# Matmuls on a tile of zeros ahead of and between the first transposes of a two-layer encoder

## The chip, the cores and the metric

The kernel runs on one core of a Trainium2 chip. A core has five engines that run side by side, each with a queue of its own, and tell each other by semaphores when a result is there: TensorE (PE: matmuls and transposes, with weight loads of its own, PEld), VectorE (DVE), ScalarE (ACT), GpSimd (POOL) and SyncE (SP), which issues most of the transfers. TensorE writes to PSUM, a memory of eight banks here, from which VectorE and ScalarE read; everything else lies in SBUF. The metric is the device time of one execution in microseconds (us). The span of a profile goes from the first to the last instruction and is a little shorter.

## The reference

A two-layer encoder over 512 tokens of 1024 channels. Each layer normalizes the tokens, mixes them along the sequence, adds a mixture of 32 experts (top 2 of one group of 8) and a gated embedding. The change lies at the very start of layer 0, in this part:

```python
def rmsnorm(x, g):
    x32 = x.astype(jnp.float32)
    y = x32 * lax.rsqrt(jnp.mean(x32 * x32, axis=-1, keepdims=True) + EPS)
    return (y * g.astype(jnp.float32)).astype(x.dtype)

def short_conv_mixer(xn, w_in, conv_w, w_out):
    bgate, cgate, h = jnp.split(xn @ w_in, 3, axis=-1)
    u = depthwise_conv(cgate * h, conv_w, (1, 1))
    return (bgate * u) @ w_out
...
    h = x
    for i in range(DEPTH):
        xn = rmsnorm(h, norm_mix[i])
```

## The kernel before

The 512 tokens are four token tiles `t` of 128. For each, the start does four things. ScalarE squares the row and sums it in two halves (`square`, L443), GpSimd makes the reciprocal root in three operations of one column (L445, L449, L450), VectorE multiplies row, root and gain in two halves (`normed`, L460), and TensorE transposes 128x128 pieces, four at a time, into an auxiliary PSUM bank (`turned`, L466). Then `turn_dense` splits the bank into two parts that together carry the full precision: ScalarE copies a rounded part (L472), VectorE subtracts it from the bank (L473). The auxiliary banks are a pool of three, `aux`; a bank comes free when L473 has read it. Weights are split likewise, by ScalarE (L147) and VectorE (L158), one half of a loaded slot at a time (`W.pump`).

A product is then three matmuls (`three`, L484 to L486: rounded by rounded, rounded by rest, rest by rounded). `begin` starts the first projection before all tokens are there. It takes two weight tiles and does the product of each with tokens 0 to 255, then with tokens 256 to 511: 24 matmuls of 256 columns in each of the four groups. Through its hook, `arrive(0)` turns token tiles 0 and 1 and issues the normalization of tiles 2 and 3 (`settle(1)`) ahead of the first group; `arrive(1)` turns tiles 2 and 3 between the first group and the second. Nothing reorders an engine's instructions: each queue runs in the order in which the code was written, waits included, so that the second group stands behind all transposes of tiles 2 and 3 on TensorE though it multiplies tokens 0 to 255 alone.

VectorE's queue at this place is: L460 for tile 0 and for tile 1, L473 twice for tile 0, L158, L473 twice for tile 1, L158, L460 for tile 2 and for tile 3, and L473 four times for both. GpSimd's is L445, L449 and L450 for each tile in turn, and ScalarE's: squares of tiles 0 and 1, L472 twice, L147, L472 twice, L147, squares of tiles 2 and 3, L472 four times.

Of the kernel before, what the change touches and what calls it, by code (L numbers as in the profile page):

```python
# [12 lines left out]
BF = mybir.dt.bfloat16  # L13
# [8 lines left out]
P = 128  # L22
# [197 lines left out]
def hybrid_encoder(ctx, tc, A, out):  # L220
    nc = tc.nc
# [7 lines left out]
    bnd = {}  # L229
# [11 lines left out]
    def aux(shape, dt=F32):  # L241
        return psum.tile(shape, dt, name="aux", tag="aux", bufs=3)
# [226 lines left out]
    def turn_dense(t, xn):  # L469
        for a in range(2):  # L470
            ps = turned(xn, a)
            nc.scalar.copy(X.hi[a][:, t], ps)  # L472
            nc.vector.tensor_tensor(X.lo[a][:, t], ps, X.hi[a][:, t], op=ALU.subtract)  # L473
# [774 lines left out]

    W.open(base[:WSP], dense_end[0])
    xns = {}  # L1250

    def arrive(n):
        for t in (2 * n, 2 * n + 1):
            turn_dense(t, xns[t])
            if n == 0:
                W.pump(1)
        if n == 0:
            settle(1)

    def settle(n):  # L1260
        for t in (2 * n, 2 * n + 1):
            square(t, 0)
            square(t, 1)
            xns[t] = normed(t, g0)

    settle(0)
    begin(2, [(0, 2), (2, 4)], arrive)
    W.pump()
    const_setup()
# [136 lines left out]
```

## Time and profile before

| | us |
|---|---|
| median of 3 executions | 1576.45 |
| the three | 1573.3, 1576.45, 1577.18 |
| profiled execution: its time | 1572.59 |
| profiled execution: its span | 1570.6 |
| TensorE busy in the span | 1487.9 (95%) |
| VectorE / ScalarE / GpSimd busy | 691.4 / 375.2 / 183.2 |

TensorE's busy time counts matmuls that overlap in its pipeline as busy, so the 95% say where it waits, not how fast it works. The mean granted clock of the span is 0.991 of full. The longest wait of TensorE in the whole span is the 8.4 us at its start.

### The profile page before, as it was taken

The numbers are of one execution on the slowest core, as the hardware profiler recorded it, in microseconds if no ns is written. First come the engines' busy times: TensorE is split into PE (matmuls) and PEld (weight loads), VectorE is DVE, ScalarE is ACT, GpSimd is POOL, SyncE is SP. The second block draws the span as 40 slices with busy tenths as digits, with TensorE's granted clock in tenths as the row PEclk, the third lists the DMA queues.
The fourth block names the chain that finished last, engine by engine and source line by source line (L and its number), as shares of the span: only waits on it lengthen the run. The fifth ranks groups of instructions, "written<-read, shape, count | busy, mean of one in ns | idle before, by whom it ended". The sixth has DMA issues, their size and how long they took to land. (4 is left out here: it accounts for less than half of the span.)

```text
span 1570.6 us, 19212 instructions
## 1 busy us (share of the span) xinstructions
PE 1487.9 (95%) x7510; PEld 896.9 (57%) x7510; DVE 691.4 (44%) x1165; ACT 375.2 (24%) x686; POOL 183.2 (12%) x271
## 2 busy tenths in 40 slices
PE   6999989999999999999898899899999999998997
PEld 5888865445444554436686678554454445544366
DVE  4554362323333332236779974623233333232266
ACT  4222231101011111015356653211011011110043
POOL 3300040000000000001346531400000000000011
PEclk9999999999999999999999999999999999999999
DMA  9432559989999999997122246599899999998951
GB/s 308 127 99 89 214 184 349 393 330 412 412 411 404 386 385 379 379 415 260 55 81 81 81 134 232 204 346 395 327 412 412 413 399 391 388 367 332 410 197 54
DMA packets 130100, 457.35 MB, mean 291 GB/s; under 512 B 11845, under 2 KB 36629, under 8 KB 113621
## 3 DMA queue, kind: packets, MB, share of 16 engines
q1 hardware_dynamic: 128036, 450.22, 74.9%
q0 software_dynamic: 1824, 5.58, 1.1%
q8 instruction: 62, 1.02, 0.3%
q14 instruction: 34, 0.27, 0.0%
q10 hardware_dynamic: 144, 0.26, 0.0%
HBM read 453.91 MB, written 2.10 MB: 290 GB/s over the span
## 5 line engine op out<-in xcount | busy, mean ns | idle before, releaser
L987 PE MATMUL acc<-slot_base,ht 128*64 128x512 f32 x728 | 205.9, 595 | 0.0
L967 DVE TENSOR_TENSOR hh<-acc,sl 128x256 f32<-128x256 f32 x64 | 39.7, 620 | 369.0 <-ACT sl L965 369.0
L860 DVE TENSOR_TENSOR h<-aux,h 128x512 f32<-128x512 f32 x256 | 161.2, 681 | 72.8 <-PE aux L858 72.8
L868 DVE SCALAR_TENSOR_TENSOR y_base<-acc,ws,y_base 128x512 fp32r<-128x512 f32 x64 | 48.1, 751 | 195.1 <-ACT y_base L867 192.3
L961 PE MATMUL acc<-slot_base,xt_xt 128*64 128x512 f32 x592 | 132.3, 592 | 0.0
L961 PE MATMUL acc<-slot_base,xt_base 128*64 128x512 f32 x528 | 119.9, 593 | 1.2 <-DMA slot_base<-in_w_exp_up_dram 1.2
L965 ACT ACTIVATE sl<-acc 128x256 f32<-128x256 f32 x64 | 24.5, 383 | 397.5 <-PE acc L961 397.5
L857 PE MATMUL aux<-y_base,marks 128*128 128x512 f32 x256 | 111.3, 435 | 8.1 <-ACT xt_base L927 2.9
L867 ACT ACTIVATE y_base<-acc,ws 128x512 fp32r<-128x512 f32 x64 | 44.0, 687 | 304.1 <-issue 227.2
L987 PEld LDWEIGHTS acc<-slot_base,ht 128*64 128x64 f32 x728 | 62.9, 137 | 88.4 <-issue 81.2
L858 PE MATMUL aux<-y_base,marks 128*128 128x512 f32 x256 | 101.6, 397 | 0.8 <-DVE y_base L868 0.6
L961 PEld LDWEIGHTS acc<-slot_base,xt_xt 128*64 128x64 f32 x592 | 42.4, 137 | 84.1 <-issue 81.1
L961 PEld LDWEIGHTS acc<-slot_base,xt_base 128*64 128x64 f32 x528 | 37.9, 137 | 77.3 <-issue 75.0
L857 PEld LDWEIGHTS aux<-y_base,marks 128*128 128x128 f32 x256 | 48.0, 187 | 58.3 <-issue 24.3
L485 PE MATMUL acc<-x_x,pair_base 128*128 128x512 f32 (+1 forms) x208 | 78.6, 378 | 1.0 <-DVE x_x L473 1.0
L484 PE MATMUL acc<-x_x,pair_base 128*128 128x512 f32 (+1 forms) x208 | 78.8, 379 | 0.0
L486 PE MATMUL acc<-x_x,pair_base 128*128 128x512 f32 (+1 forms) x208 | 78.4, 377 | 0.0
L919 PE MATMUL aux<-marks,x_z 128*128 128x256 f32 x256 | 67.1, 299 | 3.4 <-DVE h L860 2.4
L445 POOL TENSOR_SCALAR ss<-ss 128x1 f32<-128x1 f32 x28 | 8.8, 314 | 512.6 <-ACT junk L443 512.5
L486 PE MATMUL acc<-pair_base,x_z 128*128 128x512 f32 (+1 forms) x164 | 64.0, 390 | 1.0 <-DVE x_z L481 1.0
L484 PE MATMUL acc<-pair_base,x_z 128*128 128x512 f32 (+1 forms) x164 | 64.5, 394 | 0.1
L920 PE MATMUL aux<-marks,x_z 128*128 128x256 f32 x256 | 63.9, 286 | 0.1
(289 smaller groups left out, 2833.5 us busy)
## 6 DMA issues: line engine op xcount, KB each, us to landing
slot_base<-in_w_exp_down_dram SPq DMA_DIRECT2D x91, 1024.0 KB, 12.2
slot_base<-in_w_exp_gate_dram SPq DMA_DIRECT2D x140, 512.0 KB, 10.2
slot_base<-in_w_exp_up_dram SPq DMA_DIRECT2D x140, 512.0 KB, 10.2
slot_late<-in_w_exp_down_dram SPq DMA_DIRECT2D x20, 1024.0 KB, 12.6
slot_late<-in_w_exp_gate_dram SPq DMA_DIRECT2D x36, 512.0 KB, 10.3
slot_late<-in_w_exp_up_dram SPq DMA_DIRECT2D x36, 512.0 KB, 10.4
slot_early<-in_w_exp_gate_dram SPq DMA_DIRECT2D x29, 512.0 KB, 10.2
slot_early<-in_w_exp_up_dram SPq DMA_DIRECT2D x29, 512.0 KB, 10.2
```

The source lines that it names most:

```text
L484: nc.tensor.matmul(ps, lh, rh, start=first, stop=False)
L485: nc.tensor.matmul(ps, lh, rl, start=False, stop=False)
L486: nc.tensor.matmul(ps, ll, rh, start=False, stop=last)
L857: nc.tensor.matmul(ps, sg[:, t * P:(t + 1) * P], yh[:, n * 512:(n + 1) * 512], start=True, stop=False)
L858: nc.tensor.matmul(ps, sg[:, t * P:(t + 1) * P], yl[:, n * 512:(n + 1) * 512], start=False, stop=True)
L860: nc.vector.tensor_tensor(hv, ps, hv, op=ALU.add)
L867: nc.scalar.activation(yh[:, sl], yps[n], AF.Copy, scale=ws)
L868: nc.vector.scalar_tensor_tensor(yl[:, sl], yps[n], ws, yh[:, sl], op0=ALU.mult, op1=ALU.subtract)
L919: nc.tensor.matmul(ps[:, kk], X.h(t, k), rv, start=(t == 0), stop=False)
L920: nc.tensor.matmul(ps[:, kk], X.l(t, k), rv, start=False, stop=(t == T - 1))
L961: nc.tensor.matmul(ps[hf * C:(hf + 1) * C].rearrange("p (g f) -> p g f", g=2), xt[:, k, lo:lo + C], rv[:, :, kk, hf * 256:(hf + 1) * 256], ...
L987: nc.tensor.matmul(yps[n][a * C:(a + 1) * C], hts[a][:, j, half], rv[:, j, n * 512:(n + 1) * 512], start=(half == 0 and j == 0), stop=(hal ...
```

## The change

A tile of 128x512 zeros, `warm`, is made by VectorE in the pool that holds the first normalized tokens. `spin(n)` takes one auxiliary bank and multiplies the zeros with themselves into it n times, 512 columns each. Nobody reads the bank. There are 16 such matmuls ahead of everything else on TensorE, four behind the transposes of token tile 0, and four behind those of token tile 1. Nothing is removed.

```diff
--- before.py
+++ after.py
@@ -1248,11 +1248,21 @@
 
     W.open(base[:WSP], dense_end[0])
     xns = {}
+    warm = bnd["pool"].tile([P, 512], BF, name="warm")
+    nc.vector.memset(warm, 0.0)
+
+    def spin(n):
+        ps = aux([P, 512])
+        for j in range(n):
+            nc.tensor.matmul(ps, warm[:, :P], warm, start=(j == 0), stop=(j == n - 1))
+
+    spin(16)
 
     def arrive(n):
         for t in (2 * n, 2 * n + 1):
             turn_dense(t, xns[t])
             if n == 0:
+                spin(4)
                 W.pump(1)
         if n == 0:
             settle(1)
```

On TensorE, at the start of the program (`ident` is the identity of the transposes, `xn` the normalized tokens, `aux` the bank), the transposes of token tile 0 and the first of tile 1 stood so before:

```order
L466 MATMUL aux<-ident,xn 128x128 [waits DVE_49]
L466 MATMUL aux<-ident,xn 128x128 x3
L466 MATMUL aux<-ident,xn 128x128 [waits DVE_49]
L466 MATMUL aux<-ident,xn 128x128 x3
L466 MATMUL aux<-ident,xn 128x128 [waits DVE_49]
L466 MATMUL aux<-ident,xn 128x128 x3
```

Now they stand behind 16 pairs of weight load and matmul on `warm`, and tile 0's transposes are followed by four such pairs (one is shown), then tile 1's:

```order
L466 MATMUL aux<-ident,xn 128x128 [waits DVE_49]
L466 MATMUL aux<-ident,xn 128x128 x3
L466 MATMUL aux<-ident,xn 128x128 [waits DVE_49]
L466 MATMUL aux<-ident,xn 128x128 x3
L1257 LDWEIGHTS warm
L1257 MATMUL aux<-warm 128x512 [waits PE_49]
...
L466 MATMUL aux<-ident,xn 128x128 [waits DVE_49,PE_49]
L466 MATMUL aux<-ident,xn 128x128 x3
L466 MATMUL aux<-ident,xn 128x128 [waits DVE_49]
L466 MATMUL aux<-ident,xn 128x128 x3
```

Tile 1's first transposes got a wait for TensorE's own spin; their second piece waits for a VectorE instruction as before.

Still on TensorE, the second piece of tile 1 and the first matmuls of the first weight tile's group before (the numbers behind `x_x` and `pair_base` are buffers):

```order
L466 MATMUL aux<-ident,xn 128x128 [waits DVE_49]
L466 MATMUL aux<-ident,xn 128x128 x3
L484 MATMUL acc<-x_x_82,pair_base_187 128x256 [waits Activation_49]
L485 MATMUL acc<-x_x_84,pair_base_187 128x256 [waits DVE_49]
L486 MATMUL acc<-x_x_82,pair_base_187 128x256
```

And now, with four pairs on `warm` (one is shown, then the group's first three matmuls):

```order
L466 MATMUL aux<-ident,xn 128x128 [waits DVE_49]
L466 MATMUL aux<-ident,xn 128x128 x3
L1257 LDWEIGHTS warm
L1257 MATMUL aux<-warm 128x512 [waits DVE_49]
...
L484 MATMUL acc<-x_x_82,pair_base_211 128x256 [waits Activation_49]
L485 MATMUL acc<-x_x_84,pair_base_211 128x256 [waits DVE_49]
L486 MATMUL acc<-x_x_82,pair_base_211 128x256
```

The pair's first matmul waits for VectorE, since its bank is the one that token tile 0's second piece was read from. On VectorE, the start of its queue now reads as follows, with the memset of `warm` (counted in 32-bit words) behind the three that were there and ahead of the first L460:

```order
L335 MEMSET rows 128x128
L364 MEMSET mhalf 128x1
L366 MEMSET minus 128x1
L1252 MEMSET warm 128x256
L460 SCALAR_TENSOR_TENSOR xn<-h,ss,gain 128x512 [waits DMAHW1_49,DMAHW0_49,Pool_49]
L460 SCALAR_TENSOR_TENSOR xn<-h,ss,gain 128x512
```

The queues of ScalarE, GpSimd and SyncE hold the same instructions in the same order as before.

## Rows read from the trace of the kernel before

**Rows 1.** Windows: stretch and length, busy time by engine (instructions), granted clock, DMA.
```profile
15.00:20.00 5.00, 4.27 (x20) 4.27 (x21) 3.92 (x6) 3.88 (x10) 2.84 (x5) 1.00 0.54 160
...
50.00:100.00 50.00, 50.00 (x223) 41.39 (x222) 21.76 (x25) 13.50 (x18) 11.93 (x30) 1.00 0.38 119
```
**Rows 2.** Order of time, TensorE, 0 to 27 us: start, us, instruction, count, idle before.
```profile
8.35 2.21 PE L466 MATMUL aux<-ident,xn 128*128 128x128 f32 x8 [8.35 <-DVE xn L460]
...
13.40 1.12 PE L466 MATMUL aux<-ident,xn 128*128 128x128 f32 x4 [0.56 <-DVE x_x L473]
...
15.73 0.58 PE L485 MATMUL acc<-x_x,pair_base 128*128 128x256 f32 x1 [1.00 <-DVE x_x L473]
...
19.31 0.41 PE L486 MATMUL acc<-x_x,pair_base 128*128 128x256 f32 x1
19.52 0.41 PE L484 MATMUL acc<-x_x,pair_base 128*128 128x256 f32 x1
...
20.25 0.28 PE L485 MATMUL acc<-x_x,pair_base 128*128 128x256 f32 x1
20.37 0.28 PE L486 MATMUL acc<-x_x,pair_base 128*128 128x256 f32 x1
20.49 1.04 PE L466 MATMUL aux<-ident,xn 128*128 128x128 f32 x8
22.79 0.63 PE L466 MATMUL aux<-ident,xn 128*128 128x128 f32 x4 [1.26 <-DVE xn L460]
24.38 0.66 PE L466 MATMUL aux<-ident,xn 128*128 128x128 f32 x4 [0.96 <-DVE x_x L473]
24.79 0.36 PE L484 MATMUL acc<-x_x,pair_base 128*128 128x256 f32 x1
```
**Rows 3.** Order of time, ScalarE, 0 to 27 us.
```profile
14.56 0.58 ACT L472 CAST x_x<-aux 128x512 fp32r<-128x512 f32 x1 [1.09 <-PE aux L466]
...
25.08 0.59 ACT L472 CAST x_x<-aux 128x512 fp32r<-128x512 f32 x1 [1.03 <-PE aux L466]
```
**Rows 4.** Order of time, VectorE, 0 to 27 us.
```profile
0.94 0.17 DVE L335 MEMSET rows<- 128x128 f32 x1 [0.94 <-PEq L1395]
...
7.16 2.23 DVE L460 SCALAR_TENSOR_TENSOR xn<-h,ss,gain 128x512 f32<-128x512 f32 x2 [6.04 <-POOL ss L450]
10.53 2.22 DVE L460 SCALAR_TENSOR_TENSOR xn<-h,ss,gain 128x512 f32<-128x512 f32 x2 [1.14 <-POOL ss L450]
12.67 1.27 DVE L473 TENSOR_TENSOR x_x<-aux,x_x 128x512 fp32r<-128x512 f32 x2
...
15.00 1.27 DVE L473 TENSOR_TENSOR x_x<-aux,x_x 128x512 fp32r<-128x512 f32 x2
16.20 1.20 DVE L158 TENSOR_TENSOR pair_base<-slot_base,pair_base 128x1024 fp32r<-128x1024 f32 x1
18.48 2.28 DVE L460 SCALAR_TENSOR_TENSOR xn<-h,ss,gain 128x512 f32<-128x512 f32 x2 [1.08 <-POOL ss L450]
21.51 2.22 DVE L460 SCALAR_TENSOR_TENSOR xn<-h,ss,gain 128x512 f32<-128x512 f32 x2 [0.75 <-POOL ss L450]
23.63 1.89 DVE L473 TENSOR_TENSOR x_x<-aux,x_x 128x512 fp32r<-128x512 f32 x3
```
**Rows 5.** Order of time, GpSimd, 0 to 27 us.
```profile
5.46 0.23 POOL L445 TENSOR_SCALAR ss<-ss 128x1 f32<-128x1 f32 x1 [4.05 <-ACT junk L443]
...
16.80 0.70 POOL L445 TENSOR_SCALAR ss<-ss 128x1 f32<-128x1 f32 x1 [6.30 <-ACT junk L443]
...
18.53 1.20 POOL L445 TENSOR_SCALAR ss<-ss 128x1 f32<-128x1 f32 x1
...
20.91 0.57 POOL L450 TENSOR_TENSOR ss<-ss,mhalf 128x1 f32<-128x1 f32 x1
```
**Rows 6.** Order of time, TensorE, two matmuls of the second layer's mixer.
```profile
835.90 0.79 PE L484 MATMUL acc<-uh,pair_base 128*128 128x512 f32 x1 [2.31 <-DVE u L641]
...
895.72 0.50 PE L484 MATMUL acc<-uh,pair_base 128*128 128x512 f32 x1 [2.74 <-DVE yraw L703]
```

## The prediction

> **What bounds the kernel now.** I read the page first: the span is 1570.6 us (the table above), and the profiled execution took 1572.59 us, 1.99 us more than its span. The change touches only the first tokens, so next come the stages, and of them the one that prints the granted clock. From 15 to 20 us it shows 20 matmuls in 5 us, and from 50 to 100 us a TensorE that is busy for the whole 50 us [rows 1]. So behind the start TensorE is the bound for a long while: what it gains or loses before about 25 us is carried on from there. The question is whether the start of that dense work moves.
>
> The order of time on TensorE [rows 2] shows the start. TensorE is idle for 8.35 us, then transposes the tokens of tiles 0 and 1 in pieces, and from 15.73 us it does the first weight tile's 24 matmuls of 256 columns back to back. Those start 0.21 us apart (19.31, 19.52) and, from about 20 us, 0.12 us apart (20.25, 20.37). [...] The granted clock of that stretch is printed as 1.00 all the same; here I believe the starts, since the same shape can't take two times at one clock. So the transposes before 20 us and 20 of these matmuls ran at the lower level. Then follow 16 transposes of token tiles 2 and 3 (from 20.49 us, with waits), and at 24.79 us the second weight tile's matmuls begin, after which nothing stops TensorE.
>
> What starts that second group is the point of it all, so I followed it back. Its last transposes start at 24.38 us, released by VectorE's L473 [rows 2]. On VectorE [rows 4] that L473 is the run at 23.63, which stands behind L460 (the normalization of token tile 3) at 21.51; this waited for GpSimd's L450, which began at 20.91 [rows 5]. GpSimd had gone without a pause through L450 of tile 2 into L445 of tile 3 at 18.53, and VectorE's L460 of tile 2 waited for that L450 until 18.48. So the second group hangs on VectorE and GpSimd by turns, and not on TensorE.
>
> One thing is to be seen in [rows 5]: L445 is a 128x1 operation that takes 0.23 us at 5.46, but 0.70 us at 16.80 and 1.20 us at 18.53. The second ends at 17.50, just behind VectorE's L158 (16.20 to 17.40); the third at 19.73, behind the first half of the L460 that began at 18.48 and lasts 2.28 us for two. GpSimd's small operation stood still until VectorE's instruction was over.
>
> **The change part by part.**
>
> *The memset.* 128x256 words on VectorE, behind its three first memsets. The 128x128 one took 0.17 us [rows 4], so I estimate 0.34 us, up to about 1.5 us. VectorE then waits until 7.16 us: 6.04 us of cover, cost 0. Without the cover it would cost its 0.34 us.
>
> *The 16 matmuls ahead of all.* TensorE waits for nothing else until 8.35 us. No row shows this tile multiplied. Its 512 columns cost at most 0.43 us at the lower level (twice 0.213) and at least 0.24 us at the upper (twice 0.12): 16 of them 6.8 or 3.8 us, from 1.5 us to between 5.3 and 8.3 us. Both ends lie before 8.35, so no delay. I take a value between, since the first ramp here rose after some 4 us of dense work [rows 2]: about 6.5 us, and the clock up by then.
>
> *The four after token tile 0.* They stand between its 8 transposes and those of tile 1, which wait for VectorE's L460 (from 10.53, two halves in 2.22 us, so the first at about 11.65) [rows 4]. Tile 0's transposes end at 10.56 when slow [rows 2]; four matmuls take 0.96 to 1.7 us more: 11.5 or 12.3. In the fast case they are done before tile 1's tokens are there, in the slow one tile 1 starts some 0.6 us late. That doesn't reach the next step: the second half of tile 1 waits for L473 at 12.67 to 13.3 [rows 4] in any case and starts at 13.40.
>
> *The banks.* The spins take turns in the pool of three auxiliary banks, so I looked for a new wait. The order shows that tile 1's first transposes now also wait for TensorE's own spin, that its second half waits for the same VectorE instruction as before, and that the third spin waits for tile 0's second L473, which ends at 13.94. The first real matmul is held by L473 from 15.00 and comes at 15.73 anyway. No new wait on the path.
>
> *The four after token tile 1.* They follow the transposes that begin at 13.40: at the lower level 14.5 + 1.7 = 16.2 us, 0.5 us behind 15.73; at the upper 14.05 + 0.96 = 15.0, hidden.
>
> *The matmuls that now run fast.* The first weight tile's group: from 15.73, 23 starts at 0.120 instead of mostly 0.213 us; the last starts at 18.5 instead of 20.37. TensorE saves about 1.9 us there. Then it waits: token tile 2 comes from VectorE's L460 at 18.48, whose first half is done near 19.6.
>
> *The transposes that now run fast.* From their start to ScalarE's copy they take 14.56 - 13.40 = 1.16 us at the lower level and 25.08 - 24.38 = 0.70 at the upper [rows 2, 3]. ScalarE's work of that place, and the squares of tile 2 behind it, could come 0.46 us sooner, and GpSimd's L445 at 16.34 instead of 16.80. But VectorE's L158 starts at 16.20, since its own queue sets it (L473 at 15.00 twice, then L158) [rows 4], so L445 would again stand until 17.40. Then L450, L460 at 18.48, and all that hangs on it: not moved. What is late next is nothing; the saved 1.9 us turn into TensorE waiting for VectorE's L460.
>
> *Sum.* Memset 0, spins 0 (bounds: 0 and +0.5 us), first group -1.9 us on TensorE, given back whole, ScalarE's lead 0 (bounds -0.46 and 0). The second group starts at 24.8 us; the span stays 1570.6 us, within 0.5 us. The executions of before are 1572.59 (the profiled one), 1573.3, 1576.45 and 1577.18 us, with a mean of 1574.9; the median of the three timed ones is 1.6 us above that. With no change I put the new median between the two, at **1575.6 us**. About 0.3% (4.7 us) is what a measurement of this kernel can tell from no change.
>
> **The rivals.**
>
> *The early end counts (faster).* If the second group were held by TensorE's own queue, all of the 1.9 us would pass, with the 0.46: down to -2.4 us. Against it stand the waits that VectorE ended at 22.79 and 24.38 [rows 2] and the GpSimd chain. For a small part of it (0.1 to 0.46 us) speaks that L445 at 16.34 misses L158's start by only 0.14 us. 1573.2 us.
>
> *The clock falls back (slower).* The first group now ends near 18.6 us, and to 24.8 us there are only 16 transposes, a lull of 6 us, where before dense work had just ended at 20.4. After a wait of 2.31 us at 835.90 the next matmul of 512 columns took 0.79 us; after one of 2.74 us at 895.72 it took 0.50 [rows 6]. The first came at a lower clock than the second. So waits of this size sometimes drop it. The longest that I expect here is 1.4 us, with the transposes between. It decides if the second group at 24.79 starts 0.213 us apart. Then the ramp of 15.73 to 20 us is paid there: 20 times 0.093 = 1.9 us, on the path, and up to twice that if the clock comes back late, 3.8 us. 1577.5 us, at worst 1579.4.
>
> [...]
>
> *The change doesn't do what it says.* No row shows whether products of zeros raise the clock. If they don't, or if it has fallen again by 15.73, the first group runs at 0.213 us, behind a spin that ends at 16.2: it ends 0.5 us late at about 21 us, and tile 2's transposes are still done before 22.8 us, when tile 3's first half is there. The second group starts as before. 0 to +0.5 us, 1575.9 us.
>
> **How the numbers follow.** Forecast 0.76, early end 0.08, clock falls back 0.09, no effect 0.07. No case reaches 4.7 us by its own price; what is left is scatter, since the executions of before lie 4.6 us apart, and I lean the two sides evenly but for a little. Faster 0.04, same 0.92, slower 0.04. The range goes from the fast rival taken from the lowest timed execution (1573.3 - 2.4 = 1570.9) to the slow one at its worst (1579.4).
>
> **What would show it.** Right: spins from 1.5 us, their starts first 0.43 and then 0.21 to 0.24 us apart before 8.35; the 24 matmuls from 15.7 us 0.12 us apart and over by 18.6; a TensorE wait for L460 of 1 us or more behind them; VectorE's L460 at 18.5 and 21.5 and the second group at 24.8, each within 0.3 us. Wrong: L460 of tile 2 before 18.2; a first group at 0.21 us; a second group that starts at 0.21 us; or a tile 1 transposed later than 13.5. The time would be wrong if later stages lost or won more than the start moves, which no row here suggests.

## The result and the profile after

The change makes the kernel slower. The median is 1582.77 us (five executions, 1581.51 to 1584.62), and the ratio to the kernel before is 1.0055 (95% interval 1.0037 to 1.0073): some 8.7 us (the two medians alone lie 6.3 us apart), where no change was forecast and a range up to 1579.4. The profiled execution took 1581.51 us, its span is 1579.5 us (before: 1570.6), so 8.9 us of it can be looked for in the trace.

The start first: TensorE's order of time after the change, which answers to [rows 2].

```profile
1.46 5.63 PE L1257 MATMUL aux<-warm 128*128 128x512 bf16 x16 [1.46 <-DVE warm L1252]
8.17 0.66 PE L466 MATMUL aux<-ident,xn 128*128 128x128 f32 x4 [1.08 <-DVE xn L460]
...
9.74 1.03 PE L1257 MATMUL aux<-warm 128*128 128x512 bf16 x4
...
13.46 0.66 PE L466 MATMUL aux<-ident,xn 128*128 128x128 f32 x4 [0.96 <-DVE x_x L473]
...
15.79 0.39 PE L485 MATMUL acc<-x_x,pair_base 128*128 128x256 f32 x1 [0.59 <-DVE x_x L473]
...
18.53 0.28 PE L486 MATMUL acc<-x_x,pair_base 128*128 128x256 f32 x1
19.79 0.63 PE L466 MATMUL aux<-ident,xn 128*128 128x128 f32 x4 [0.98 <-DVE xn L460]
...
22.67 1.11 PE L466 MATMUL aux<-ident,xn 128*128 128x128 f32 x4 [1.23 <-DVE xn L460]
24.34 1.12 PE L466 MATMUL aux<-ident,xn 128*128 128x128 f32 x4 [0.56 <-DVE x_x L473]
25.11 0.56 PE L484 MATMUL acc<-x_x,pair_base 128*128 128x256 f32 x1
...
25.89 0.41 PE L484 MATMUL acc<-x_x,pair_base 128*128 128x256 f32 x1
26.11 0.41 PE L485 MATMUL acc<-x_x,pair_base 128*128 128x256 f32 x1
```

The warm-up does what it says: four transposes take 0.66 us already at 8.17, and the first group runs from 15.79 to 18.53. Then TensorE waits 0.98 us for VectorE. But the transposes at 22.67 take 1.11 us again, and the second group starts its matmuls 0.22 us apart (25.89, 26.11). The windows of the same kernel say when:

```profile
20.00:25.00 5.00, 2.85 (x15) 1.98 (x14) 4.26 (x6) 1.76 (x3) 1.35 (x2) 0.76 1.06 356
25.00:30.00 5.00, 5.00 (x28) 5.00 (x27) 1.17 (x2) 2.48 (x3) 2.90 (x2) 0.56 1.09 348
...
650.00:655.00 5.00, 1.28 (x9) 1.22 (x10) 1.55 (x5) 0.00 (x0) 0.00 (x0) 0.91 1.02 403
655.00:660.00 5.00, 4.37 (x20) 4.14 (x20) 0.00 (x0) 1.23 (x3) 0.00 (x0) 0.50 1.02 406
```

The granted clock is 0.76 and 0.56 there, and the five microseconds from 25 hold 28 matmuls. VectorE's split of one and the same weight half, before and after:

```profile
31.91 1.23 DVE L158 TENSOR_TENSOR pair_base<-slot_base,pair_base 128x1024 fp32r<-128x1024 f32 x1 [5.52 <-ACT pair_base L147]
```
```profile
34.13 1.23 DVE L158 TENSOR_TENSOR pair_base<-slot_base,pair_base 128x1024 fp32r<-128x1024 f32 x1 [7.33 <-ACT pair_base L147]
```

So **2.2 us** are lost at the start. They stay 2.2 us until 200 us; 0.4 us more come in at two transposes near 204 and 212 us, and then the loss stays at 2.6 us until 648 us. The last two windows show a second place, late in layer 0's experts, and there the loss jumps. VectorE's row of one and the same copy, before and after:

```profile
654.03 0.69 DVE L925 COPY xt_base<-aux 128x512 f32<-128x512 f32 x1 [4.21 <-PE aux L920]
```
```profile
661.94 0.69 DVE L925 COPY xt_base<-aux 128x512 f32<-128x512 f32 x1 [9.49 <-PE aux L920]
```

661.94 - 654.03 = 7.91 us, less the 2.6 that were there, so **5.3 us** come in there. TensorE's order of time at the place, of the kernel before:

```profile
648.16 0.58 PE L940 MATMUL aux<-wx,R 128*128 128x6 f32 x4 [1.21 <-DVEq L1072]
648.60 0.37 PE L919 MATMUL aux<-marks,x_z 128*128 128x256 f32 x1
...
652.47 0.28 PE L919 MATMUL aux<-marks,x_z 128*128 128x256 f32 x1
652.89 0.39 PE L920 MATMUL aux<-marks,x_z 128*128 128x256 f32 x1
```

And after:

```profile
650.79 0.58 PE L940 MATMUL aux<-wx,R 128*128 128x6 f32 x4 [1.21 <-DVEq L1072]
...
651.79 0.28 PE L919 MATMUL aux<-marks,x_z 128*128 128x256 f32 x1
655.63 0.37 PE L920 MATMUL aux<-marks,x_z 128*128 128x256 f32 x1 [3.57 <-issue]
655.81 0.42 PE L919 MATMUL aux<-marks,x_z 128*128 128x256 f32 x1
656.02 0.41 PE L920 MATMUL aux<-marks,x_z 128*128 128x256 f32 x1
```

This L940 is the first work behind the overflow loop, which handles tokens beyond an expert's 64 slots. Here there are none, and TensorE jumps over the loop's body. Before, the matmuls behind the jump run on, but for 0.3 us between 652.47 and 652.89. After, TensorE stops for 3.57 us in the middle of a run of equal matmuls whose operands are there; nothing released it ("issue"). The clock falls in that pause (granted 1.00 from 653 to 654 us, 0.54 from 654 to 655 and 0.50 from there to 660), and the matmuls behind it start 0.21 us apart (655.81, 656.02) instead of 0.12, half rate. At this L940 the loss is still 2.6 us (648.16 and 650.79). In layer 1 both kernels wait at the L940 behind the jump: 5.8 us before, 6.1 after, in the view of TensorE's waits. The rows of before and after read:

```profile
PE aux L940 <- issue: 5.8, 1, 5.8
```
```profile
PE aux L940 <- PEq L1072: 6.1, 1, 6.1
```

The last 1.0 us of the 8.9 comes in later, as a balance of gains and losses.

**The theories.** A: the place of the code. The profile lists transfers of a queue "instruction" (62 packets, 1.02 MB), and the theory takes them to bring TensorE its instructions. The change puts 48 instructions ahead of the jump, 24 pairs of weight load and matmul (47 more by the trace's records, since one wait fell away). That would move the border up to which instructions are there when the jump lands. Counted from L940, before has 4 + 16 + 4 + 9 = 33 pairs until its gap, after has 4 + 5 = 9: exactly 24 fewer. B: it is all the start; the clock that fell at 22.6 us costs 2.2 us, which later collisions enlarge.

### The profile page after: what moved, and what is told of

It reads as the page before. It is cut to its first block, busy times and chain, and to the rows that moved or that the text cites. A ratio compares the mean times of both kernels' runs of the same rounds, so it can differ in the third digit from the quotient of the medians.

```text
span 1579.5 us, 19260 instructions
## 1 busy us (share of the span) xinstructions
PE 1497.3 (95%) x7534; PEld 901.6 (57%) x7534; DVE 691.9 (44%) x1166; ACT 375.2 (24%) x686; POOL 182.4 (12%) x271
## 3 DMA queue, kind: packets, MB, share of 16 engines
q8 instruction: 62, 1.02, 0.3%
## 5 line engine op out<-in xcount | busy, mean ns | idle before, releaser
L987 PE MATMUL acc<-slot_base,ht 128*64 128x512 f32 x728 | 205.9, 595 | 0.0
L987 PEld LDWEIGHTS acc<-slot_base,ht 128*64 128x64 f32 x728 | 62.9, 137 | 88.3 <-issue 81.8
L919 PE MATMUL aux<-marks,x_z 128*128 128x256 f32 x256 | 68.8, 304 | 3.2 <-DVE h L860 2.5
L920 PE MATMUL aux<-marks,x_z 128*128 128x256 f32 x256 | 65.5, 291 | 3.6 <-issue 3.6
L445 POOL TENSOR_SCALAR ss<-ss 128x1 f32<-128x1 f32 x28 | 9.0, 320 | 516.9 <-ACT junk L443 516.9
```

The costliest lines, as they stand in the source:

```text
L919: nc.tensor.matmul(ps[:, kk], X.h(t, k), rv, start=(t == 0), stop=False)
L920: nc.tensor.matmul(ps[:, kk], X.l(t, k), rv, start=False, stop=(t == T - 1))
L987: nc.tensor.matmul(yps[n][a * C:(a + 1) * C], hts[a][:, j, half], rv[:, j, n * 512:(n + 1) * 512], start=(half == 0 and j == 0), stop=(hal ...
```

## The experiments

Ratios are to the kernel before, with 95% intervals; the columns at the right are from the profiles. "Left" is the number of pairs from the jump's target to the border, counted in layer 0.

| run | median us | ratio | left | wait in layer 0, us | wait in layer 1, us |
|---|---|---|---|---|---|
| before | - | 1 | 33 | 0.3 | 5.8 |
| the change | 1582.77 | 1.0055 (1.0037 to 1.0073) | 9 | 3.57 | 6.1 |
| 24 small pairs | 1582.14 | 1.0039 (1.0024 to 1.0054) | 8 | 3.73 | 6.1 |
| spins moved into the lull | 1582.93 | 1.0047 (1.0033 to 1.006) | 10 | 3.3 | 6.0 |
| spins cut in four | 1571.4 | 0.9976 (0.9965 to 0.9987) | far | 1.2 | 1.2 |
| 85 small pairs | 1567.95 | 0.9947 (0.9933 to 0.9961) | far | 1.2 | 1.2 |
| 128 small pairs | 1576.01 | 0.9998 (0.9986 to 1.001) | 32 | 0.22 | 6.0 |
| 12 small pairs | 1579.81 | 1.0016 (1.0005 to 1.0028) | 20 | 2.12 | 6.2 |
| the change behind 62 small pairs | 1570.97 | 0.9965 (0.9951 to 0.9979) | far | 1.2 | 1.2 |
| before, without the jump | 1568.41 | 0.9949 (0.9935 to 0.9964) | - | none | none |
| the change, without the jump | 1569.22 | 0.9957 (0.9941 to 0.9972) | - | none | none |

(1.2 us is the wait for the count that decides the jump. Every kernel with the jump has it in layer 0; where another number stands, it is a wait on top of this or, in layer 1, in its place. These are put down to "issue", but the four of layer 1 in the change, the 24 and the 12 small pairs and the spins moved to L1072, TensorE's own jump. The 0.3 of before is read from two starts.)

**24 small pairs, no warm-up.**

```diff
+    for j in range(24):
+        nc.tensor.matmul(ps[:P, :2], warm[:, :P], warm[:, :2], start=(j == 0), stop=(j == 24 - 1))
```

> The kernel before, with 24 pairs of weight load and matmul on zeros of 2 columns each ahead of the first transposes: as many TensorE instructions as the change adds, but hardly any work. Theory A (the place of the code: 48 more instructions ahead of the skipped overflow loop move the border up to which the instructions behind the jump have been fetched, so that TensorE runs dry there): the start as before, second group at 24.8 us at 0.12 us a matmul; near 651 us a TensorE wait of about 3.6 us that nothing releases, with half rate behind it; 5 to 6 us slower than before. Theory B (all of the loss comes from the clock that falls at 22.6 us and the 2.2 us that it costs, passed on and grown by later collisions): no wait at 651 us, the time of before within 2 us.

Measured: 1.0039, so 6.1 us slower, with the second group at full rate (it starts at 25.21, its matmuls 0.12 us apart). TensorE's order of time:

```profile
653.68 0.37 PE L919 MATMUL aux<-marks,x_z 128*128 128x256 f32 x1 [3.73 <-issue]
```

A's wait is there without the warm-up, behind the eighth pair, since this kernel has two instructions more than the change. B has no explanation for it.

**The spins moved into the lull.** As many matmuls as the change: 12 ahead, 2 and 2 behind tiles 0 and 1, then

```diff
+        if n == 1:
+            spin(4)
...
+            elif t == 2:
+                spin(4)
```

> The change with its 24 matmuls on zeros put elsewhere: 12 ahead of all, 2 behind token tile 0, 2 behind tile 1, 4 ahead of tile 2's transposes and 4 behind them. The instructions are as many as in the change. Both theories: the clock holds through the lull, the second group runs at 0.12 us a matmul from about 24.3 to 24.8 us, so the 2.2 us of the start are gone. Theory A: the wait of 3.6 us near 651 us stays with its half rate; about 2.5 us faster than the change, 5 us slower than before. Theory B: with the start repaired the time of before, within 2 us, and no wait at 651.

Measured: 1.0047; the wait at 651 us stays (3.3 us). The second group does run at full rate (0.12 us apart), but no earlier than it would:

```profile
24.52 1.09 PE L466 MATMUL aux<-ident,xn 128*128 128x128 f32 x8 [1.33 <-DVE x_x L473]
25.36 0.36 PE L484 MATMUL acc<-x_x,pair_base 128*128 128x256 f32 x1
25.57 0.28 PE L485 MATMUL acc<-x_x,pair_base 128*128 128x256 f32 x1
25.68 0.29 PE L486 MATMUL acc<-x_x,pair_base 128*128 128x256 f32 x1
```

The new spins took a bank, so that all of tile 3's transposes now wait for L473. The start is 0.6 us later than before, not earlier. That the run would be 2.5 us faster than the change was not seen: 1.0047 against 1.0055 lies inside the intervals. This run speaks for A by its wait and leaves the price of the start open.

**The spins cut in four**, 192 added instructions with the same columns:

```diff
-        for j in range(n):
-            nc.tensor.matmul(ps, warm[:, :P], warm, start=(j == 0), stop=(j == n - 1))
+        for c in range(4):
+            cs = slice(c * P, c * P + P)
+            for j in range(n):
+                nc.tensor.matmul(ps[:, cs], warm[:, :P], warm[:, cs], start=(j == 0), stop=(j == n - 1))
```

> The change with each matmul on zeros cut into four of 128 columns: the same columns at the same places, but 192 added instructions instead of 48. Theory A: the start as in the change (clock up early, down near 22.6 us, 2.2 us lost), but the border now lies far behind the jump in layer 0 (no wait near 651 us) and, as counted in the built program, also behind the one in layer 1, where the kernel before waits 5.8 us at 1431 us: about 2 to 4 us faster than before, 10 to 12 faster than the change. Theory B: the time of the change, 8 us slower than before.

Measured: 0.9976, 3.8 us faster than before, though the start shows the change's fault, a second group at half rate (0.21 us apart) from 25.11 us:

```profile
25.46 0.41 PE L485 MATMUL acc<-x_x,pair_base 128*128 128x256 f32 x1
...
25.89 0.41 PE L484 MATMUL acc<-x_x,pair_base 128*128 128x256 f32 x1
```

The same columns of zeros in four times as many instructions turn a loss into a gain. B falls with this.

**85 small pairs, no warm-up.** As the 24, with 85 pairs of 32 and 2 columns; the number is from a count of the built program. There the jump skips 305 of TensorE's instructions in either layer. If borders lie 256 apart (assumed here; the run with 128 small pairs bears it out) and the one of layer 0 lies at the gap of before, layer 1's border lies a few instructions behind the jump's target. 171 more would move both borders far behind it.

> The kernel before with 85 pairs of weight load (32 columns) and matmul (2 columns) on zeros ahead of the first transposes: 170 more instructions, chosen so that by the count in the built program the border lies behind both jumps. Theory A: no wait near 651 us, and the 5.8 us at 1431 us shrink to about the 1.2 us that layer 0 waits there, with no half rate behind: 5 to 7 us faster than before. Theory B: the time of before within 2 us.

Measured: 0.9947, 8.4 us faster than before, more than the 5 to 7 us expected. The waits for L940 are the count's alone, two of 1.2 us:

```profile
PE aux L940 <- DVEq L1072: 2.4, 2, 1.2
```

The half rate in layer 0 is there all the same (0.21 us apart from 650.12 us), without a stop ahead of it; the granted clock is 0.66 in this window:

```profile
650.00:655.00 5.00, 5.00 (x31) 4.64 (x30) 0.12 (x1) 1.23 (x3) 0.00 (x0) 0.66 1.03 403
```

From L940 to the next L987 it takes 6.5 us, against 5.4 in the run with the spins cut in four. So the half rate behind the stop of the change can't be put down to the stop alone.

**128 small pairs**, 257 more instructions:

> As the 85 pairs, but 128 pairs: 256 more instructions and one memset. Theory A (the border comes back every 256 TensorE instructions): everything as in the kernel before again, a wait of 0.3 us near 652 us, one of about 5.8 us at 1431 us, and the time of before within 0.3%. Rival (more instructions, or more small work at the start, make what follows better whatever their number): as with the 85 pairs or better, 6 us or more faster than before.

Measured: 0.9998. The old gap is back, behind the 32nd pair, and so is layer 1's wait:

```profile
PE aux L940 <- issue: 6.0, 1, 6.0
...
PE aux L919 <- issue: 0.2, 1, 0.2
```

So it isn't that more small work helps; with 257 more instructions the effect is back.

**12 small pairs.**

> As the 24 pairs, but 12 pairs: half of the shift. Theory A in its graded form (the wait is what the instructions between the jump's target and the border don't cover: 0.3 us with 33 pairs of matmul and load left in the kernel before, 3.6 us with 9 left in the change, so 0.136 us for each pair): a wait of about 1.9 us near 651 us; 1.6 us slower than before if the clock holds, 3.5 us if it falls; the wait at 1431 us as before, about 6 us. Rival (the wait is there or not, a fetch that comes in time or is lost): 0.3 or 3.6 us.

Measured: 1.0016, 2.5 us slower. The break comes behind the 20th pair, and the wait is between the ends:

```profile
654.73 0.83 PE L974 MATMUL aux<-ident,hh 128*128 128x128 f32 x4 [2.12 <-issue]
```

2.12 us with 20 pairs left, where the line through before and after (0.136 us for a pair) gives 2.1: the wait is graded, as what the remaining instructions don't cover. (The 1.9 us expected were for 21 pairs.) The neighbours of the change say the same: 3.3 us with 10 pairs left, 3.57 with 9, 3.73 with 8. The rival of this run (there or not) is out.

**What the traces say of the place.** Six kernels stop in layer 0: before, the change, the 24, 12 and 128 small pairs, and the spins moved. Counted over all instructions that TensorE ran, the one that comes late is the 6549th in five of them, though up to 49 instructions more stand ahead of the jump, and the 6805th, 256 later, with 128 small pairs. The place is fixed in the program, and the jump moves against it. The late instruction comes 6.0 to 6.2 us behind the jump in layer 0 and 6.1 to 6.3 us in layer 1, in all six. Each time one 16 KB transfer of the queue "instruction" starts 3.5 to 3.7 us behind the jump and ends 1.3 to 1.5 us before the late instruction; in the change it ran from 653.03 to 654.11 us, and TensorE went on at 655.63. That the queue serves TensorE is inferred from its packets: 62 before, 63 in the four runs with 170 or more TensorE instructions added. So the stop behind the target and the wait at the target are one thing: what TensorE lacks is there some 6 us behind the jump, and it waits for as much of that as its remaining instructions don't fill.

**The change behind 62 small pairs**, in the places of the 85:

```diff
-    spin(16)
+    spin(16, 62)
```

where `spin(n, few)` begins with `few` matmuls of 2 columns in its bank.

> The change as it is, with 62 pairs of 32 and 2 columns on zeros put ahead of its first 16 matmuls, in the same bank: its instructions now stand in the same places as those of the run with 85 pairs. What is left between the two is the warm-up alone. Theory A: no wait at either jump; the clock rises early, falls near 22.6 us, and the second group is 2.2 us late: 2 to 2.5 us behind the 85 pairs, so about 4.5 us (0.3%) faster than before. Theory B: 8 us slower than before.

Measured: 0.9965, against 0.9947 for the 85 pairs: 0.0018 of 1577 us are 2.8 us for the warm-up alone, though the two intervals overlap. In its profile the clock fell later than in the change, behind 22.6 us (the transposes at 24.27 took 1.12 us, those at 22.61 took 0.66), and the second group's loss is 1.3 us. It had also fallen for a while near 14 us (granted 0.77 from 15 to 20 us, where the change ran its first group at full rate), so this warm-up is not the change's in every detail.

**Without the jump**, both kernels; the loop is left out, and with it the work for tokens beyond the slots, of which there are none here:

```diff
-                    overflow(self.i, self.ex, self.wo, self.yspot, self.sgs)
```

> The kernel before without the overflow loop of both layers and its jumps: what is left out is the work for tokens beyond an expert's 64 slots, of which there is none in these executions, and the reading of the count that decides it. Theory A: TensorE waits neither the 1.2 us at 647 us nor the 5.8 us at 1431 us, and the half rate behind the latter is gone: 8 to 11 us faster than before. Theory B gives no gain beyond the two waits for the count, 1.2 us each: 2 to 3 us.

> The change without the overflow loop of both layers and its jumps, the same part left out as in the other run. Theory A: with no jump the place of the code is of no account; no wait near 651 and 1439 us, and what is left between this and the other run is the start alone, 1.3 to 2.2 us: 6 to 9 us faster than before. Theory B: as far behind the other run as the change is behind before, 8 us.

Measured: 0.9949 and 0.9957, 8.0 and 6.8 us faster than before. With no jump the change costs 0.0008, 1.3 us; the intervals of the two overlap. So the warm-up's own price is 1.3 us by one comparison and 2.8 by another, each with intervals that overlap, and most of the 8.7 us needs the jump.

Of the kernels that do all of the reference's work, the one with the 85 small pairs has the lowest ratio, with one memset and 170 idle instructions more than before.

## Why the prediction was wrong

**What held.** The chain that sets the second group was read rightly. VectorE's normalizations, which answer to [rows 4], hardly moved:

```profile
18.51 2.22 DVE L460 SCALAR_TENSOR_TENSOR xn<-h,ss,gain 128x512 f32<-128x512 f32 x2 [1.04 <-POOL ss L450]
21.47 2.21 DVE L460 SCALAR_TENSOR_TENSOR xn<-h,ss,gain 128x512 f32<-128x512 f32 x2 [0.74 <-POOL ss L450]
```

GpSimd's L445 came 0.41 us sooner and stood until L158 was over (17.46 and 17.55 us), as said; answering to [rows 5]:

```profile
16.39 1.16 POOL L445 TENSOR_SCALAR ss<-ss 128x1 f32<-128x1 f32 x1 [5.84 <-ACT junk L443]
```

The memset (0.27 us), the 16 matmuls (over by 7.1), the banks, the third spin and the first group's 1.9 us, all given back, were right in place and nearly in size. The two rates that I read from the starts go with the granted clock elsewhere in these profiles: 0.21 us apart at 0.50 (the change, 656 to 660 us), 0.12 us apart at 1.00 (before, 25 to 30 us).

**The clock through the lull: a rival taken for unlikely.** It had a chance of 0.09 and a price of 1.9 us; it came, at 2.2 us in the profiled execution. What I weighed wrongly was the row of a wait of 2.74 us after which the clock held (granted 1.00 from 895 to 900 us) [rows 6]. Here no single wait was over 1.23 us, and still it fell (granted 0.76 from 20 to 25 us, 0.56 from 25 to 30): between 18.6 and 22.6 us TensorE had only eight transposes. Before, the dense group, most of it 0.21 us apart, ended at 20.4 us, and the clock then held (granted 1.00 from 20 to 30 us). What makes it fall, the runs don't tell: here it fell with waits of 0.98, 0.37 and 1.23 us and transposes between them, there it held over one of 2.74 us.

**The sum: the step that failed.** "Memset 0, spins 0 (bounds: 0 and +0.5 us)" costed the added instructions by their time and their waits, where they stand. 5.3 us of the profiled loss come in 600 us later: 3.3 us of wait (3.57 less the 0.3 of before), which their number brings about, and the remaining 2.0 us at half rate behind it. Without the jump the change costs 1.3 us instead of 8.7. The range had no room for it, and "which no row here suggests" was wrong: the wait of 5.8 us for "issue" at layer 1's L940 stood in the view of TensorE's waits that I had read, and I did not ask what it was. That row was the kernel before paying the same price in layer 1.

The runs show the price in two forms. In layer 1 of the change, the 24 and 12 small pairs and the spins moved, the first instruction behind the jump is the late one, and TensorE waits 6.0 to 6.2 us. Where the first instructions behind the jump run, the stop comes later and is shorter: 0.3, 2.12 and 3.57 us with 33, 20 and 9 pairs left, and 5.8 us in layer 1 of the kernel before, where TensorE ran three instructions behind the jump and then stopped. With 128 small pairs, 257 more instructions, the stops of before are back, at 0.22 and 6.0 us.

**Left open.** The last 1.0 us of the profiled 8.9 is not explained; its largest step, some 1.6 us, lies near 900 us, where the granted clock is 0.50 from 900 to 905 us in the change and was 1.00 at that place before. Why the clock fell at 650 us with 85 small pairs, without a stop, is not known either, nor whether it would have fallen in the change without one. Why the clock fell at 22.6 us in the change and later in the run behind 62 small pairs, with the same matmuls in the same order, the runs don't tell. That the transfer of instructions releases the late one is inferred from the counts and times, which agree in all twelve stops; no view shows the release. Why it starts only 3.5 us behind the jump, no run shows.

## What to carry to other kernels

Where a program jumps at run time, count instructions as well as time. Here 48 instructions ahead of the jump brought 3.3 us more of wait behind it, and nearly empty ones moved the kernel both ways (1.0039 with 24 pairs, 0.9947 with 85), so that a change that measures as a gain or a loss may be this alone; a run with the same number of idle instructions separates the two. Read every wait that nothing releases, in the kernel before too: of the 5.8 us here the 85 pairs left 1.2. And the early warm-up was worth nothing here, where VectorE sets the start of the second group (TensorE waited 1.23 us for it at 22.67 us), and cost 2.2 us in the profiled execution, when the clock fell in the pause that it opened.

## What the runs showed of the hardware that was not expected

TensorE paused 0.2 to 3.7 us in the middle of equal matmuls behind a jump over 305 instructions (by the count in the built program), graded by what was left to the border, and about 6 us at the target itself; with 128 small pairs the late instruction stood 256 later (6805 against 6549). The late instruction came 6.0 to 6.3 us behind the jump in all twelve stops. In the change the clock fell in such a pause (0.50 from 655 to 660 us), and 3.3 us of pause went with 2.0 us at half rate; with 85 small pairs it fell at the same place without one (0.66 from 650 to 655 us).
